# A chunked delta-rule scan: the end decay on the new values (ScalarE) in place of the keys (GpSimd)

## Chip, cores and metric

The kernel runs on one core of a Trainium2 chip. The metric is the device time of one execution in microseconds (us), the median of several. Engines are named PE (TensorE, matrix products), DVE (VectorE), ACT (ScalarE), POOL (GpSimd) and SP (SyncE, which issues most transfers).

## The reference

One layer of a hybrid backbone over 2048 latent tokens with a prefix of 256 context tokens: a mixer of two head groups (a chunked gating MLP and a bidirectional gated delta rule), and then a mixture of 16 experts. The part that matters here is the scan of the delta rule. Per direction, head (4 of 128) and chunk it carries a 128x128 state:

```python
g_last = gcum[..., -1]
k_g = kc * jnp.exp(g_last[..., None] - gcum)[..., None]

def step(state, xs):
    q_i, k_i, u_i, w_i, a_i, gl_i = xs
    v_new = u_i - w_i @ state
    o_i = q_i @ state + a_i @ v_new
    state = state * jnp.exp(gl_i)[..., None, None] + jnp.swapaxes(k_i, -1, -2) @ v_new
    return state, o_i
```

`k_g` is the key of a token times the decay from that token to the end of its chunk, a factor per token and head. In the product of keys and new values the token is the index that is summed over, so the factor may stand on either of the two.

## The kernel before

The kernel has four stages, written one after the other: the input projection with its convolution; the gating MLP, together with the preparation and the triangular solves of the delta rule; the scan, together with the output projection and the router; and the experts. The diff touches the scan alone (`scan`, L979 to L1038).

The scan works on chunks of 128 tokens, 18 of them (2 of context, 16 latent), in both directions at once: step s takes one chunk for the forward and one for the backward direction, so there are 18 steps and 36 scans. `scan` is a generator that yields between its products; `drive` (L866) takes one piece from each direction in turn, and, as a third generator, one from `finish` (L791 to L864), which assembles the inverse matrices for the next step out of what the solve has left (its products are L827, L835, L846, L848, L853 and L860; between them ACT and DVE evict, in L830, L839, L849, L854 and L863, and POOL multiplies by a mask in L822). From step 10 on each step also feeds `out_norm`, `out_proj` and `out_route` (L1040 to L1156) with two finished chunks.

For one chunk and one direction `scan` does this. Four tiles `kv` are loaded through SP (L986): keys `kr`, values `vr`, and transposed keys `kT` and queries `qT`; there are 12 buffers of the kind, and a buffer goes back when its last reader is done. POOL multiplies `kr` by EGK, the decay to the end of the chunk, one column per head (L988, 128x512, in place). PE multiplies `kT` with the state (L993), DVE subtracts (L995, one instruction per head), PE multiplies with the inverse UF (L1000), and DVE scales the result to the new values `vn` (L1006, or L1004 in the first step; one instruction for all heads). PE forms the state product of `kr` and `vn` (L1010, one matmul per head, two instructions to a matmul), and DVE adds it to the decayed state (L1016, or L1013 in the first step). For latent chunks PE then forms the queries' product with the old state (L1025) and the local one (L1029, which reads `vn` too), ACT copies (L1031) and DVE adds (L1033). The PSUM tiles `ks` of all these products share three buffers; `vn` has two.

The engines each work in the order of a list. A planner fixes it before the run: it takes the instructions in the order of the program, with a reckoning of the time that each takes, and places one of them on its engine when its inputs and a buffer are reckoned to be there. So PE's pieces of both directions, of `finish` and of the output projection are interleaved by the planner and not by the text of the program.

Beside the scan, in the same stretch of time: the last of the triangular solves (`solve`, L750 to L777) runs on DVE, 30 rounds of a product into `tmp` (L765) and a sum into `U` (L767) for each direction, all operands in SBUF; `load_wo` (L963) prepares the output weights, with two products per piece on POOL (L973 and L975) and a copy on ACT between them (L974); and the last chunks of the gating MLP (L660 to L713) use ACT, among others for a scaling by a column, four heads of 128x128 (L689). `rpow` (L164) is a small power on POOL.

## Time and profile before

| | us |
|---|---|
| median of 3 runs | 2490.56 |
| lowest, highest | 2490.39, 2495.03 |
| the profiled execution | 2486.87 |
| its span in the trace | 2485.1 |
| PE busy in the span | 2359.3 (95%) |
| DVE busy | 1577.9 (63%) |
| ACT busy | 1119.7 (45%) |
| POOL busy | 492.7 (20%) |

The times in the trace count from the start of the span. The scan's first products run at 758 us, its last at 1220 us. A row of the timeline gives the start, the length, the engine, the line and the operation, the tiles written and read, and how many instructions were merged into the row; in brackets stands the time that the engine was idle before it and what ended that. A busy share over the whole span is a mean over stages with different limits; a table by windows of the span shows each stage by itself. Such a row gives the window, its length, the busy time of PE, of PE's weight loads, of DVE, ACT and POOL (with the number of instructions), the clock that TensorE was granted as a share of 2.4 GHz, the mean busy share of the 16 DMA engines, and GB/s.

### The profile page before, as it was taken

What the parts mean: (1) busy time and instruction counts of PE and PEld (TensorE: products, weight loads), DVE (VectorE), ACT (ScalarE), POOL (GpSimd) and SP (SyncE); (2) the same over time, 40 slices, a digit from 0 to 9 for tenths busy, and PEclk for the clock granted to TensorE, in tenths of its full rate; (3) what the DMA queues carried; (4) which work ended last, traced back from release to release, by engine and by line L of the source; (5) the groups of instructions that cost most, each with busy time, mean ns of one, the idle gap of its engine ahead of it and who ended that gap; (6) DMA issues with size and microseconds to landing.
All of it is one profiled execution on the core that took longest, in us unless ns stands there. A gap on an engine that the chain in (4) does not pass through costs nothing.

```text
span 2485.1 us, 43121 instructions
## 1 busy us (share of the span) xinstructions
PE 2359.3 (95%) x16841; PEld 2156.1 (87%) x16841; DVE 1577.9 (63%) x3339; ACT 1119.7 (45%) x2008; POOL 492.7 (20%) x447
## 2 busy tenths in 40 slices
PE   7999999999988899999949999999999999999998
PEld 5999999887777888888838899999999999998888
DVE  7788755368779556576774556555565565556675
ACT  5554545567633343333332444444444444444553
POOL 1222212111102543232250101101111010011211
PEclk9999999999988999999978999999999999999999
DMA  9756735499856997555563667666676666668894
GB/s 288 229 191 220 239 123 171 144 290 299 260 120 195 264 270 231 189 188 174 174 189 111 204 187 224 195 206 205 204 221 195 212 213 197 208 208 262 311 304 161
DMA packets 487994, 526.59 MB, mean 212 GB/s; under 512 B 103887, under 2 KB 409880, under 8 KB 485742
## 3 DMA queue, kind: packets, MB, share of 16 engines
q1 hardware_dynamic: 470238, 463.27, 59.2%
q0 software_dynamic: 17120, 59.77, 8.3%
q8 instruction: 133, 2.18, 0.4%
q10 hardware_dynamic: 432, 0.79, 0.1%
q14 instruction: 71, 0.58, 0.1%
HBM read 400.45 MB, written 123.31 MB: 211 GB/s over the span
## 4 chain that ended last, share of the span: by engine, by line
PE 48%; DMA 9%; DVE 3%; issue 2%; ACT 2%; POOL 1%; SPq 0%; POOLq 0%; DVEq 0%; ACTq 0%
PE gu L196 7%; PE gu L195 7%; PE gu L194 7%; PE dn L194 4%; PE dn L195 4%; PE dn L196 4%; DMA xg<-f_rows,idx 4%; PE mx L194 2%; PE mx L196 2%; PE mx L195 2%; ACT wh L183 1%; PE xt L1381 1%; DVE wl L184 1%; DMA raw<-in_w_gate_dram 1%; DMA raw<-in_w_down_dram 1%
## 5 line engine op out<-in xcount | busy, mean ns | idle before, releaser
L184 DVE TENSOR_TENSOR wl<-raw,wh 128x2048 fp32r<-128x2048 f32 (+1 forms) x218 | 459.6, 2118 | 292.7 <-ACT wh L183 292.4
L194 PE MATMUL gu<-xS,wh 128*128 128x256 f32 x2048 | 581.3, 285 | 5.1 <-ACT wh L183 3.3
L196 PE MATMUL gu<-xS,wl 128*128 128x256 f32 x2048 | 579.2, 285 | 5.8 <-DVE wl L184 5.8
L195 PE MATMUL gu<-xS,wh 128*128 128x256 f32 x2048 | 580.9, 284 | 0.0
L183 ACT ACTIVATE wh<-raw 128x2048 fp32r<-128x2048 f32 (+1 forms) x218 | 381.6, 1771 | 360.6 <-DMA raw<-in_w_gate_dram 144.3
L194 PEld LDWEIGHTS gu<-xS,wh 128*128 128x128 f32 x2048 | 394.5, 193 | 7.5 <-ACT wh L183 4.2
L196 PEld LDWEIGHTS gu<-xS,wl 128*128 128x128 f32 x2048 | 393.1, 193 | 7.5 <-DVE wl L184 6.5
L195 PEld LDWEIGHTS gu<-xS,wh 128*128 128x128 f32 x2048 | 394.8, 193 | 1.1
L194 PE MATMUL pj<-aS,wh 128*128 128x258 f32 x832 | 236.6, 287 | 3.8 <-DVE y L460 2.4
L195 PE MATMUL pj<-aS,wh 128*128 128x258 f32 x832 | 238.5, 287 | 0.6 <-DVE aS L358 0.5
L196 PE MATMUL pj<-aS,wl 128*128 128x258 f32 x832 | 237.1, 286 | 0.8 <-DVE wl L184 0.8
L194 PE MATMUL dn<-wh,hS 128*128 128x512 f32 (+1 forms) x520 | 202.7, 390 | 0.0
L195 PE MATMUL dn<-wl,hS 128*128 128x512 f32 (+1 forms) x520 | 201.1, 387 | 0.0
L196 PE MATMUL dn<-wh,hS 128*128 128x512 f32 (+1 forms) x520 | 200.3, 386 | 0.0
L1458 POOL DMA_INDIRECT h_rows<-ye,idx x26 | 62.9, 2418 | 659.3 <-DVE ye L1421 567.0
L194 PEld LDWEIGHTS pj<-aS,wh 128*128 128x128 f32 x832 | 156.5, 189 | 5.2 <-ACT wh L183 1.8
L195 PEld LDWEIGHTS pj<-aS,wh 128*128 128x128 f32 x832 | 157.7, 190 | 1.3 <-DVE aS L358 1.0
L196 PEld LDWEIGHTS pj<-aS,wl 128*128 128x128 f32 x832 | 156.9, 189 | 1.3 <-DVE wl L184 1.1
L194 PE MATMUL uv<-wh,ast 128*128 128x512 f32 x384 | 155.7, 405 | 0.0
L196 PE MATMUL uv<-wh,ast 128*128 128x512 f32 x384 | 152.5, 397 | 0.0
L195 PE MATMUL uv<-wl,ast 128*128 128x512 f32 x384 | 152.2, 396 | 0.0
L1404 ACT ACTIVATE hS<-sgl 128x256 fp32r<-128x256 f32 x128 | 53.0, 414 | 184.1 <-DVE sgl L1402 183.9
(480 smaller groups left out, 4519.6 us busy)
## 6 DMA issues: line engine op xcount, KB each, us to landing
raw<-in_w_gate_dram SPq DMA_DIRECT2D x64, 1024.0 KB
raw<-in_w_up_dram SPq DMA_DIRECT2D x64, 1024.0 KB
raw<-in_w_down_dram SPq DMA_DIRECT2D x64, 1024.0 KB
kv<-kv SPq DMA_DIRECT2D x140, 256.0 KB
raw<-in_w_mod_dram SPq DMA_DIRECT2D x18, 1024.0 KB
a_sp<-aS SPq DMA_DIRECT2D x32, 512.0 KB
ast<-a_sp POOLq DMA_DIRECT2D x16, 1024.0 KB, 8.0
raw<-in_w_in_dram SPq DMA_DIRECT2D x12, 1024.0 KB
```

Of the source, the lines that this page charges most:

```text
L183: nc.scalar.activation(wh[:, ks, s:s + 256], raw[:, ks], AF.Copy)
L184: (lo_eng or nc.vector).tensor_tensor(wl[:, ks, s:s + 256], raw[:, ks], wh[:, ks, s:s + 256].bitcast(F32), op=OP.subtract)
L194: pace(nc.tensor.matmul(ps, ah, bh, start=(k == 0), stop=False), after)
L195: nc.tensor.matmul(ps, ah, bl, start=False, stop=False)
L196: return nc.tensor.matmul(ps, al, bh, start=False, stop=(k == nk - 1))
L1381: nc.tensor.transpose(ps[:, k2, hf * P:(hf + 1) * P], xg[:, hf, k * P:(k + 1) * P], ident)
L1404: nc.scalar.activation(hS[0][:, ff, :], sg_, AF.Copy)
L1458: nc.gpsimd.indirect_dma_start(out=h_rows, out_offset=bass.IndirectOffsetOnAxis(ap=idx[:, hf:hf + 1], axis=0), in_=ye[:, hf, :], in_offset ...
```

## The change

The product of the keys with EGK on POOL (L988) is gone. After `vn` is computed, four ACT instructions, one per head, copy `vn` into a new tile `vk` (128x512, one buffer) and multiply by the head's column of EGK on the way. The state product reads the unscaled keys and `vk`. The local product for the output (L1029) reads `vn`, as before. Nothing else is different.

```diff
--- before.py
+++ after.py
@@ -985,7 +985,6 @@
                 kv[i] = wkv.tile([P, H, P], F32, name="kv", bufs=12)
                 nc.sync.dma_start(kv[i], kv_d[t][:, i].rearrange("p (h i) -> p h i", h=H))
             kr, vr, kT, qT = kv
-            nc.gpsimd.tensor_tensor(kr, kr, EGK[:, d, ci:ci + H][:, :, None].to_broadcast([P, H, P]), op=OP.mult)
             if not first:
                 yield
                 ks = ps_s.tile([P, H, P], F32, name="ks")
@@ -1004,10 +1003,13 @@
                 nc.vector.scalar_tensor_tensor(vn, vps, -1.0, nb, op0=OP.mult, op1=OP.mult)
             else:
                 nc.vector.tensor_tensor(vn, vps, nb, op=OP.mult)
+            vk = wks.tile([P, H, P], F32, name="vk", bufs=1)
+            for h in range(H):
+                nc.scalar.activation(vk[:, h, :], vn[:, h, :], AF.Copy, scale=EGK[:, d, ci + h:ci + h + 1])
             yield
             sp = ps_s.tile([P, H, P], F32, name="ks")
             for h in range(H):
-                nc.tensor.matmul(sp[:, h, :], kr[:, h, :], vn[:, h, :], start=True, stop=True)
+                nc.tensor.matmul(sp[:, h, :], kr[:, h, :], vk[:, h, :], start=True, stop=True)
             Sn = wks.tile([P, H, P], F32, name=f"S{d}", bufs=2)
             if first:
                 mark[0] = nc.vector.tensor_copy(Sn, sp)
```

## Rows read from the trace of the kernel before

**Rows 1.** Timeline, DVE, then PE, 749 to 772 us.

```profile
750.47 0.55 DVE L765 TENSOR_TENSOR tmp<-U 96x108 f32<-96x108 f32 x2
750.94 1.40 DVE L767 TENSOR_TENSOR U<-U,tmp 96x108 f32<-96x108 f32 x2
...
753.27 1.45 DVE L765 TENSOR_TENSOR tmp<-U 96x150 f32<-96x150 f32 x2
...
755.47 0.89 DVE L767 TENSOR_TENSOR U<-U,tmp 96x228 f32<-96x228 f32 x1
...
757.39 1.50 DVE L765 TENSOR_TENSOR tmp<-U 96x184 f32<-96x184 f32 x2
...
767.94 0.87 DVE L830 TENSOR_TENSOR raw<-kk,m 64x256 f32<-64x256 f32 x2
...
758.23 1.95 PE L1000 MATMUL ks<-kv,raw 128*128 128x128 f32 x16
768.86 1.91 PE L835 MATMUL kk<-raw 128*128 128x32 f32 x8 [8.67 <-DVE raw L830]
```

**Rows 2.** Table by windows: length, busy us per engine, clock, DMA share.

```profile
764.00:778.00 14.00, 8.57 (x44) 8.07 (x45) 13.20 (x36) 3.33 (x10) 3.88 (x4) 0.51 0.14 41
820.00:840.00 20.00, 17.85 (x165) 16.90 (x164) 9.84 (x33) 8.37 (x19) 12.78 (x8) 1.00 0.93 265
840.00:860.00 20.00, 18.04 (x123) 16.47 (x121) 7.48 (x24) 6.63 (x18) 10.49 (x7) 0.74 0.93 267
1000.00:1040.00 40.00, 40.00 (x254) 34.05 (x254) 26.65 (x66) 15.72 (x35) 10.32 (x10) 1.00 0.64 208
```

**Rows 3.** Line L988: ns min/median/max; its busy time in a window.

```profile
L988 POOL TENSOR_TENSOR kv<-kv,EGK x36: 1029/1040/1231, 750.7 to 1169.9; 128x512 f32<-128x512 f32 x36
...
750.50:758.50 8.00, 4.58 (x4) 1.00 1.05 342
```

**Rows 4.** Line L1006: ns min/median/max, first and last start.

```profile
L1006 DVE TENSOR_TENSOR vn<-ks,NBET x34: 675/690/692, 785.2 to 1200.2; 128x512 f32<-128x512 f32 x34
```

**Rows 5.** Timeline of ACT at 770 to 776 us.

```profile
772.24 1.28 ACT L689 ACTIVATE gl<-gl,rvb 128x128 f32<-128x128 f32 x4 [0.31 <-POOL rvb L164]
```

**Rows 6.** Timeline: new values vn and the state products that read them.

```profile
785.25 0.69 DVE L1006 TENSOR_TENSOR vn<-ks,NBET 128x512 f32<-128x512 f32 x1
786.28 1.14 PE L1010 MATMUL ks<-vn,kv 128*128 128x128 f32 x8
...
796.01 0.69 DVE L1006 TENSOR_TENSOR vn<-ks,NBET 128x512 f32<-128x512 f32 x1
797.05 1.14 PE L1010 MATMUL ks<-vn,kv 128*128 128x128 f32 x8
...
815.64 0.68 DVE L1006 TENSOR_TENSOR vn<-ks,NBET 128x512 f32<-128x512 f32 x1
816.48 1.13 PE L1010 MATMUL ks<-vn,kv 128*128 128x128 f32 x8 [1.56 <-DVE vn L1006]
...
831.29 2.05 PE L1010 MATMUL ks<-vn,kv 128*128 128x128 f32 x16
...
983.37 0.68 DVE L1006 TENSOR_TENSOR vn<-ks,NBET 128x512 f32<-128x512 f32 x1
989.24 1.06 PE L1010 MATMUL ks<-vn,kv 128*128 128x128 f32 x8
```

**Rows 7.** Timeline of PE: the first step's two state products.

```profile
773.93 3.62 PE L1010 MATMUL ks<-vn,kv 128*128 128x128 f32 x16
```

**Rows 8.** Waits of PE, 775 to 960 us: total us, times, longest us.

```profile
PE ks L1029 <- ACT ot L1031: 4.6, 4, 1.9
```

**Rows 9.** Timeline at 826 to 833 us, ACT and PE.

```profile
828.43 1.06 ACT L974 ACTIVATE wh<-ft 128x1024 fp32r<-128x1024 f32 x1 [4.49 <-POOL ft L973]
...
829.70 0.41 PE L846 MATMUL lv<-ident,raw 64*64 64x64 f32 x4 [2.15 <-ACT raw L839]
```

## Prediction

> **What bounds the kernel now.** I read the table by stages first, then what each engine waits for, then the timeline around the lines that the diff touches. The change lies in the scan alone, 36 scans (18 steps, two directions) between 750 and 1210 us; the other 2,000 us see none of it.
>
> The scan has three parts. From 750 to about 772 us it overlaps the last triangular solve. There VectorE works without a gap, and TensorE stands still: after the matmuls at 758.23 us the next, at 768.86, waited 8.67 us for VectorE's L830, which stands in VectorE's queue behind the solve's L765 and L767 [rows 1]. From there to about 960 us (steps 0 to 11, 24 scans) neither TensorE nor the transfers leave much room: in 820 to 840 us TensorE is busy 17.85 of 20 us and the DMA engines 0.93 of the time, while ScalarE has 8.37 of 20 us [rows 2]. From 960 us on the output projection fills in, and TensorE is busy 40.00 of 40 us [rows 2]: what comes late to one matmul there is covered by others. So what the change does is decided in the first two parts.
>
> **Part by part.** Removed: 36 products on GpSimd, 1.04 us each in the median, 37 us in all [rows 3]. No row of TensorE's waits names GpSimd; these products are work beside the path, and the 37 us are no gain in themselves. The point is what they take from others: four of them run between 750.5 and 758.5 us beside the solve [rows 3], and VectorE's rows under them are stretched. A pair of L765 takes 0.55 us just before the first, and the pair of L767 with the same shape takes 1.40 under it; the pairs at 753.27 and 757.39 take 1.45 and 1.50, and a single one at 755.47 takes 0.89 [rows 1]. Against about 0.6 for a pair and 0.4 for a single (estimates from the 0.55) that is 0.85 + 0.85 + 0.9 + 0.5 = 3.1 us. VectorE has no idle time between them and L830, and TensorE stands waiting for L830, so all of it is on the path: -3.1 us. Next late there is still L830, since 5.6 us of the wait are left.
>
> The Trainium skill, GPSIMD Engine Reference, section 1 (Specifications), says that GpSimd shares its SBUF interfaces with VectorE, and that the contention concerns VectorE instructions with two SBUF inputs or in a two-port mode. If each of the 36 products cost VectorE 0.85 us on the path, the change would give back 31 us; the trace bears the rule out for the solve, whose inputs both lie in SBUF, and not beyond it.
>
> What VectorE does in the scan itself reads one input from PSUM, and its rows don't stretch: L1006 takes 675 to 692 ns in all 34 executions, beside a GpSimd product or not [rows 4]. So the gain ends with the solve, and I take no more than the 3.1 us.
>
> Added: per scan four ScalarE copies with a scale from a column. The nearest row is the same form in the stage before: L689, 128x128 from SBUF to SBUF with a column as scale, four in 1.28 us [rows 5]. 36 x 1.28 = 46 us of ScalarE, 31 of them in the 24 early scans. ScalarE is less than half busy there, so this is no bound as such; it counts as latency and as a place in a queue.
>
> As latency: the state product L1010 waited for VectorE's vn (L1006 or L1004); now it waits for vn and then vk. Its matmuls start about 0.23 us apart (16 instructions, two to a matmul, in 2.05 us less the tail of the last [rows 6]). With 0.1 us for each of the two hand-overs (an estimate, from the 0.16 between vn's end at 816.32 and the product at 816.48 that waited for it [rows 6]) the matmul of the fourth head could start 1.48 us after vn's end; unchanged, it starts 0.7 us after the first. So a product that starts 0.8 us or more after the end of vn loses nothing, if ScalarE is free. In the late part the distance is long: vn ends at 984.05, the product starts at 989.24 [rows 6]. In the early part three scans are closer: 785.94 and 786.28, 796.70 and 797.05, and the pair at 816 us [rows 6]. They are short of 0.8 by 0.5, 0.4 and 0.6: +1.5 us. The first step's two products run at half clock, 16 instructions in 3.62 us [rows 7], 0.45 us per matmul, and heads of vk every 0.3 us keep up with that; for the copies of L689 ahead of them in ScalarE's queue I take +0.5, between 0 and 1.3 (one group).
>
> vk has one buffer, so the second direction's copies wait until the first direction's product has read it. Where the two products run back to back, as the 16 instructions at 831.29 us [rows 6], the second starts later by nothing (released head by head) or by some 0.75 us (released as a whole); three such steps lie in the early part: 0 to 2.25, I take the middle, +1.1.
>
> As a place in the queue: ScalarE works in order and carries evictions that TensorE waits for. The largest sum of such waits in the early part is 4.6 us in 4 waits, for L1031 [rows 8]. If each of the four came behind one whole group of vk, that is +5 us; if none does, 0. vk takes 1.28 us of ScalarE twice in a step of 15 us, 1/6 of the time, so I stay near the lower end: +1.0.
>
> Moved: on GpSimd's queue the product waited for a transfer of keys; L973, L975, L822 and the small powers (L164) behind it may start sooner. Since no matmul waited for them, that is nothing, or a few tenths by way of VectorE. The keys' slot goes back when the state product has read it, as before; where that product is late, the transfer that takes the slot starts later on SP's queue, with what stands behind it there, and with the DMA engines at 0.93 nothing hides it. That is why I count the latencies in full. The order of instructions comes from a planner that reckons with costs of its own; with other instructions it may put TensorE's pieces in another order, which no row prices. That goes into the range.
>
> The sum is -3.1 + 0.5 + 1.5 + 1.1 + 1.0 = +1.0 us. The profiled execution took 2486.87 us (2485.1 in the span, 1.8 around it), and the median of the runs shown is 3.7 above it. On the median: 2491.5 us, no change.
>
> **The rivals.** Slower: TensorE starves at the state product, in steps 3 to 6. There ScalarE also runs L974, which waits for GpSimd and a transfer of weights: at 828.43 ScalarE had stood 4.49 us for it, L839 behind it was late, and TensorE's L846 waited 2.15 us [rows 9]. A group of vk behind such an L974 holds up the recurrence itself. For this speaks that ScalarE has one queue in order; against it, that GpSimd without the products may finish L973 sooner. Price: one wait like those 2.15 us. It decides from the point where TensorE's clock falls for it: in 840 to 860 us the granted clock is 0.74 of full, half the stretch at 1.2 in place of 2.4 GHz, and TensorE starts 123 matmul instructions, against 165 in the 20 us before [rows 2]; 42/165 x 20 = 5.1 us lost. Together 1.0 + 2.15 + 5.1 = +8.3: about 2499 us.
>
> Faster: the wait for L830 falls from 8.67 to 5.6 us, and the half-clock time behind it goes too (0.51 granted in 764 to 778 us [rows 2]). Then the 16 instructions of the first products take 2.05 us, as at 831.29, in place of 3.62 [rows 6, 7], 1.6 us less. The other 28 of the 44 instructions in that stretch would save 0.1 us each at the same ratio, 2.7 us, of which I count half, since they also wait for other engines: 1.3. If the planner covers the added latency but for the three tight scans, the sum is -3.1 - 2.9 + 1.5 = -4.5, and with some tenths by way of VectorE about 2485 us. By the skill's rule on the shared interfaces, cited above, this is the side on which I would be wrong. Against it: 5.6 us is still a long stop.
>
> No effect: VectorE's stretch comes back from another GpSimd instruction that moves into the place (L822, which also runs beside the solve), and vk is hidden. That gives 2490.5 us, inside the forecast's band.
>
> **How the numbers follow.** Forecast and no-effect case together 0.50, the slower rival 0.28, the faster one 0.22. What a measurement of this kernel can tell from no change is about 0.2%, 5 us, so these are also the chances of same (2485.6 to 2495.5), slower and faster. From the bounds above the forecast's own range is 2488.5 to 2498 (latencies and queue at their lower ends: -3.1 + 1.5; at their upper: -3.1 + 1.3 + 1.5 + 2.25 + 5). The range that should hold 8 in 10 reaches to both rivals and a little beyond, for a planner's order that no row prices: 2482 to 2502.
>
> **What would show it.** Right: rows of L765 and L767 near 0.6 us per pair at 750 to 758 us, and L835 some 3 us earlier; four ScalarE copies in 1.28 us per scan; state products in the early steps up to 0.6 us later behind vn, none of them in the late ones; GpSimd busy 37 us less. Wrong on the slow side: a wait of TensorE's L1010 for ScalarE of over 2 us, or one more stretch at half clock before 960 us. Wrong on the fast side: full clock from 764 us on, or an early part that is shorter by more than the 3 us. The prediction falls too if the late part, where I count nothing, changes its length by more than 2 us.

## The result, and the profile after

| | before | after |
|---|---|---|
| median, us | 2490.47 | 2523.15 |
| lowest, highest (4 runs each) | 2484.31, 2495.03 | 2509.06, 2528.39 |
| ratio of the times (95% interval) | | 1.0126 (1.0101 to 1.0150) |
| the profiled execution, its span | 2486.87, 2485.1 | 2528.39, 2526.6 |
| PE, DVE, ACT, POOL busy in the span | 2359.3, 1577.9, 1119.7, 492.7 | 2383.2, 1574.0, 1164.0, 461.0 |

The change makes the kernel 33 us slower; the forecast was no change, and the range ended at 2502. Line numbers of after: L992 is the product with the state, L999 the one with the inverse, L1005 the new values, L1008 the copies into `vk`, L1012 the state product, L1018 the new state, L1027 the queries' product, L1031 the local one.

Where the time went can be read from the starts of the steps (the first product with the state in each step; the last column is a mark at the start of the experts' stage, ACT's copy into `V`, L1239, in after L1241), in us of the span:

| | step 1 | step 2 | step 6 | step 11 | steps 2 to 11 | experts |
|---|---|---|---|---|---|---|
| before | 779.5 | 789.7 | 862.6 | 943.8 | 154.1 | 1269.9 |
| after | 777.2 | 787.1 | 876.4 | 979.0 | 191.9 | 1302.2 |

After is 2.3 and 2.6 us ahead at the first two steps, falls 38 us back in the nine steps from 2 to 11, and keeps 32 of it. So the loss lies where the prediction looked for it, in the early steps, and it is not one event: steps 6 to 10 last 19 to 23 us each, against 15 to 18 before. The two profiled executions differ by 41.5 us (2526.6 and 2485.1). The other 9 lie in the experts' stage, 1224.4 and 1215.2 us long, which the change doesn't touch and which lasts 1211 to 1224 us in the kept traces of all kernels.

First the stretch ahead of the scan. Timeline of after, DVE and then PE (the rows that answer to [rows 1]):

```profile
749.01 0.55 DVE L765 TENSOR_TENSOR tmp<-U 96x108 f32<-96x108 f32 x2
749.48 0.55 DVE L767 TENSOR_TENSOR U<-U,tmp 96x108 f32<-96x108 f32 x2
...
753.73 0.65 DVE L765 TENSOR_TENSOR tmp<-U 96x184 f32<-96x184 f32 x2
...
763.43 0.86 DVE L830 TENSOR_TENSOR raw<-kk,m 64x256 f32<-64x256 f32 x2
...
764.35 1.92 PE L835 MATMUL kk<-raw 128*128 128x32 f32 x8 [6.38 <-DVE raw L830]
```

No pair of the solve takes 1.4 or 1.5 us any more. From the start of the pair L765 with 96x108 elements to the start of L830 it is 14.42 us (763.43 - 749.01); before it was 17.47 (767.94 - 750.47), so 3.05 us are gone, where 3.1 were forecast. L830 as such comes 4.5 us earlier, since this execution was 1.5 us ahead when the stretch began. PE waits 6.38 us for it in place of 8.67.

Most of that is lost again in after's first step. From the start of L830 to step 1 it is 11.6 us before (767.94 to 779.5), 11.8 in e1, which has no copies, and 13.8 after (763.43 to 777.2). There the second direction's copies wait until the first state product, at half clock there, has read the one buffer:

```profile
775.00 1.28 ACT L1008 ACTIVATE vk<-vn,EGK 128x128 f32<-128x128 f32 x4 [3.14 <-PE ks L1012]
```

Then one step of the early part. Timeline of after, DVE, ACT and PE from 880 to 893 us:

```profile
880.38 1.42 DVE L1005 TENSOR_TENSOR vn<-ks,NBET 128x512 f32<-128x512 f32 x2
885.22 1.12 DVE L1018 SCALAR_TENSOR_TENSOR S<-S,ETO,ks 128x128 f32<-128x128 f32 x4 [3.41 <-PE ks L1012]
891.53 1.12 DVE L1018 SCALAR_TENSOR_TENSOR S<-S,ETO,ks 128x128 f32<-128x128 f32 x4 [5.19 <-PE ks L1012]
...
881.49 0.56 ACT L839 ACTIVATE raw<-lv 32x128 f32<-32x128 f32 x2
882.06 0.94 ACT L819 ACTIVATE raw<-UD 32x128 f32<-32x128 f32 x3
883.03 1.28 ACT L1008 ACTIVATE vk<-vn,EGK 128x128 f32<-128x128 f32 x4
884.33 0.30 ACT L819 ACTIVATE raw<-UD 32x128 f32<-32x128 f32 x1
884.66 0.55 ACT L839 ACTIVATE raw<-lv 32x128 f32<-32x128 f32 x2
885.23 1.28 ACT L1008 ACTIVATE vk<-vn,EGK 128x128 f32<-128x128 f32 x4
...
881.81 0.41 PE L846 MATMUL lv<-ident,raw 64*64 64x64 f32 x4 [0.74 <-ACT raw L839]
883.48 1.70 PE L1012 MATMUL ks<-vk,kv 128*128 128x128 f32 x8 [1.26 <-ACT vk L1008]
885.26 1.11 PE L848 MATMUL lv<-ident,raw 64*64 64x64 f32 x8
886.30 0.79 PE L1012 MATMUL ks<-vk,kv 128*128 128x128 f32 x2
886.89 1.91 PE L1027 MATMUL ks<-S,kv 128*128 128x128 f32 x8
888.60 1.06 PE L1012 MATMUL ks<-vk,kv 128*128 128x128 f32 x4
889.45 1.82 PE L1027 MATMUL ks<-S,kv 128*128 128x128 f32 x8
891.11 0.39 PE L1012 MATMUL ks<-vk,kv 128*128 128x128 f32 x2
```

Read it from vn to the state. The new values of both directions are there at 881.80. The first copies start at 883.03, behind five instructions of `finish` (L839, L819) that stand ahead of them in ACT's list. The second start at 885.23, behind three more of these; the first state product has read the one buffer just before, at 885.18, and ACT has no idle time there, so this step doesn't tell which of the two holds them. And PE has the last two instructions of the second state product at 891.11, because all 16 instructions of the queries' products L1027 stand between its pieces. The new state is complete at 892.65, 12.3 us after the start of vn. In a step of before, from the timeline of its DVE, the same way takes 6.7 us:

```profile
881.09 0.69 DVE L1006 TENSOR_TENSOR vn<-ks,NBET 128x512 f32<-128x512 f32 x1
882.87 0.69 DVE L1006 TENSOR_TENSOR vn<-ks,NBET 128x512 f32<-128x512 f32 x1 [1.09 <-PE ks L1000]
883.77 1.12 DVE L1016 SCALAR_TENSOR_TENSOR S<-S,ETO,ks 128x128 f32<-128x128 f32 x4 [0.20 <-PE ks L1010]
...
886.64 1.12 DVE L1016 SCALAR_TENSOR_TENSOR S<-S,ETO,ks 128x128 f32<-128x128 f32 x4
```

Below I call this way, from the start of the first vn to the end of the last state row, "values to state", and give its mean over the steps between 800 and 960 us: 6.9 us before, 13.0 after. The chain from state to state runs through it. The steps of one column vary: kernels that take about the time of before have 152 to 170 us for steps 2 to 11 in the table below, so a difference under some 15 us there tells little by itself.

It also costs clock. Table by windows of after (length, busy time of PE, its loads, DVE, ACT, POOL, granted clock, DMA share, GB/s), the same step in pieces, then two longer stretches; the last row is of before:

```profile
880.00:884.00 4.00, 2.00 (x18) 1.65 (x16) 1.75 (x4) 3.65 (x13) 0.42 (x1) 1.00 0.76 228
884.00:888.00 4.00, 3.92 (x22) 3.50 (x22) 1.12 (x4) 2.81 (x10) 0.00 (x0) 0.53 0.55 135
888.00:892.00 4.00, 4.00 (x25) 4.00 (x24) 0.47 (x2) 0.00 (x0) 0.00 (x0) 0.62 0.19 66
...
780.00:960.00 180.00, 156.09 (x1207) 146.79 (x1206) 84.28 (x274) 88.45 (x249) 54.38 (x38) 0.86 0.78 225
860.00:990.00 130.00, 112.80 (x840) 105.34 (x839) 56.82 (x184) 63.42 (x184) 26.86 (x23) 0.84 0.72 216
...
780.00:960.00 180.00, 165.29 (x1471) 154.66 (x1471) 106.88 (x347) 78.78 (x213) 80.26 (x64) 0.97 0.91 261
```

PE stands for half of 880 to 884, in two stops of 0.74 and 1.26 us, and then works about 7 us at half the clock; that comes back in each of the next steps, at 863.7, 884.2, 904.7, 925.1 and 945.6 us, 6.8 us each. From 755 to 1100 us half the clock was granted for 34 us before and for 75 us after. That is 41 us more, worth 20 us of products (half of 41).

The waits in 780 to 1000 us (in total, times, the longest): DVE and PE of after, then DVE of before:

```profile
DVE S L1018 <- PE ks L1012: 75.7, 19, 7.9
...
PE ks L1012 <- ACT vk L1008: 12.8, 8, 4.0
...
DVE S L1016 <- PE ks L1010: 7.3, 9, 1.7
```

DVE waits for the state product for 75.7 us, and for 7.3 before; PE itself shows only 12.8 us of waiting for `vk`. The rest of the lateness has no row of its own on PE: it is other work placed ahead.

### The profile page after: what moved, and what is told of

Read it like the earlier page. It is cut to its first block, busy times and chain, and to the rows that moved or that the text cites. A ratio compares the mean times of both kernels' runs of the same rounds, so it can differ in the third digit from the quotient of the medians.

```text
span 2526.6 us, 43229 instructions
## 1 busy us (share of the span) xinstructions
PE 2383.2 (94%) x16841; PEld 2179.9 (86%) x16841; DVE 1574.0 (62%) x3339; ACT 1164.0 (46%) x2152; POOL 461.0 (18%) x411
## 4 chain that ended last, share of the span: by engine, by line
PE 66%; DMA 14%; DVE 9%; issue 4%; ACT 4%; POOL 2%; SPq 1%; DVEq 0%; POOLq 0%; ACTq 0%
PE gu L196 6%; PE gu L195 6%; PE gu L194 6%; DMA xg<-f_rows,idx 4%; PE dn L194 4%; PE dn L195 4%; PE dn L196 4%; PE pj L195 4%; PE pj L194 4%; PE pj L196 4%; ACT wh L183 2%; PE mx L194 2%; PE mx L196 2%; PE mx L195 2%; PE ks L1027 1%
```

## The experiments

All ratios are against the kernel before, run on the same chip beside each. "Values to state" and "steps 2 to 11" are of the profiled execution. Differences between two kernels are told in medians; by the ratios they come out up to 4 us larger or smaller.

| kernel | median us | ratio (95%) | values to state | steps 2 to 11 |
|---|---|---|---|---|
| after | 2523.2 | 1.0126 (1.0101, 1.0150) | 13.0 | 191.9 |
| e1 no scaling at all | 2486.8 | 0.9983 (0.9966, 1.0000) | 7.0 | 154.9 |
| e2 keys scaled on ACT | 2490.9 | 0.9992 (0.9973, 1.0012) | 5.5 | 165.0 |
| e14 before + unread copies | 2490.1 | 0.9990 (0.9973, 1.0006) | 5.5 | 165.3 |
| e5 copy on DVE, beside vn | 2487.9 | 0.9984 (0.9964, 1.0004) | 6.9 | 158.8 |
| e6 copy on DVE, behind vn | 2505.9 | 1.0055 (1.0036, 1.0075) | 9.6 | 183.8 |
| e7 one short copy on ACT | 2514.9 | 1.0077 (1.0051, 1.0103) | 8.9 | 178.3 |
| e4 after + redundant products | 2512.5 | 1.0085 (1.0058, 1.0112) | 9.3 | 174.0 |
| e3 after, PE's order held | 2508.0 | 1.0069 (1.0044, 1.0094) | 8.8 | 179.4 |
| e9 after, ACT's order held | 2510.0 | 1.0077 (1.0056, 1.0097) | 8.0 | 176.9 |
| e13 after, no shared buffer | 2506.6 | 1.0053 (1.0036, 1.0069) | 9.1 | 174.6 |
| e8 both orders held | 2494.4 | 1.0014 (0.9997, 1.0031) | 6.2 | 170.3 |
| e15 both orders, one short copy | 2494.6 | 1.0005 (0.9987, 1.0023) | 7.1 | 162.2 |
| e16 both orders, no shared buffer | 2487.6 | 0.9978 (0.9957, 0.9998) | 6.1 | 166.5 |
| e10 before, part of after's order on PE | 2487.5 | 0.9975 (0.9954, 0.9996) | 6.7 | 158.6 |
| e12 before, state products first | 2490.4 | 0.9991 (0.9978, 1.0005) | 4.7 | 152.5 |
| e11 e5, state products first | 2496.0 | 1.0016 (1.0001, 1.0030) | 4.7 | 155.2 |
| e17 e5 with e10's order | 2489.4 | 0.9984 (0.9965, 1.0003) | 6.4 | 154.6 |

### Which part of the change costs: e1, e2, e14, e5

e1: the kernel before without the scaling.

```diff
-            nc.gpsimd.tensor_tensor(kr, kr, EGK[:, d, ci:ci + H]..., op=OP.mult)
```

> The kernel before without the product of the keys on GpSimd and with nothing in its place: the end decay is left out of the state, so the time is that of the work without it. It takes away the GpSimd work alone. Theory of the forecast: VectorE's solve is no longer held up beside it, the finishing product L835 comes 3 us earlier, and the time is 2487 us (about 3 below before). Rival, that GpSimd's product kept the planner's order in place and that taking it away is what costs: 2505 us or more. A scan step in the early part should last 15 to 17 us by the first and about 20 us by the second.

2486.8 us beside 2491.8 of before, 5 us less at the edge of what can be told. The stretch from L765 to L830 lasts 14.42 us, as in after; in e2, e5, e8 and e16, which have no product on GpSimd either, 14.35 to 14.43; in e10, e12 and e14, which have it, 17.20 to 17.22. So the removal is a small gain, and the solve has it: steps 2 to 11 take 154.9 us, as before.

e2: the keys scaled on ACT, four copies per scan, off the path.

```diff
-            nc.gpsimd.tensor_tensor(kr, kr, EGK[:, d, ci:ci + H]..., op=OP.mult)
+            for h in range(H):
+                nc.scalar.activation(kr[:, h, :], kr[:, h, :], AF.Copy, scale=EGK[:, d, ci + h:ci + h + 1])
```

> The kernel before with the keys scaled by four ScalarE copies in place of the product on GpSimd: the same ScalarE work as in the changed kernel (144 copies, 46 us), but on the keys, which are there long before, so that nothing stands between the new values and the state product. Theory, that the latency between vn and the state product is the cause: 2487 to 2493 us, as before or a little less, with steps of 15 to 17 us. Rival, that ScalarE's added load is the cause (its queue holds up the evictions that TensorE waits for): 2510 us or more, with steps near 20 us and falls of the clock as in the changed kernel.

The same amount of ScalarE work, 144 copies ahead of the path, costs nothing that can be told: 2490.9.

e14: before, plus the change's copies at their place, read by nobody.

```diff
                 nc.vector.tensor_tensor(vn, vps, nb, op=OP.mult)
+            vk = wks.tile([P, H, P], F32, name="vk", bufs=1)
+            for h in range(H):
+                nc.scalar.activation(vk[:, h, :], vn[:, h, :], AF.Copy, scale=EGK[:, d, ci + h:ci + h + 1])
```

> The kernel before, keys scaled on GpSimd and the state product from the new values, plus the 144 scaled copies on ScalarE at the place they have after the change, which nothing reads (they are extra work; the result is the reference's). Theory (the loss is the dependence: the state product behind the copies): the copies hang beside the path, time 2488 to 2498 us. Rival (the copies push ScalarE's evictions for the solve and the outputs back, and these hold the chain): 2505 us or more.

2490.1, no loss, though steps 2 to 11 are 11 us longer in this execution; the late part takes that up. Waits of DVE in e14, 780 to 1000 us:

```profile
DVE S L1019 <- PE ks L1013: 6.7, 9, 2.1
```

6.7 us for the state product, where after has 75.7. So the copies' load on ACT, and what they push back there, is not the cause of the 33 us; that the state product reads them is.

e5: the copy made on DVE from the product `vps`, ahead of vn, with one table for both factors (NEK is NBET times EGK; the lines that make it, and the form of the first step, are left out here).

```diff
+            vk = wks.tile([P, H, P], F32, name="vk", bufs=1)
+            nc.vector.tensor_tensor(vk, vps, NEK[:, d, ci:ci + H]..., op=OP.mult)
             nc.vector.tensor_tensor(vn, vps, nb, op=OP.mult)
-            for h in range(H):
-                nc.scalar.activation(vk[:, h, :], vn[:, h, :], AF.Copy, scale=EGK[:, d, ci + h:ci + h + 1])
```

> The kernel after, with the state product's scaled copy made on VectorE straight from the product vps (times one table that holds beta and decay together) and issued ahead of the new values, so that neither GpSimd nor ScalarE has a part in it and nothing stands between the new values and the state product; the copy keeps its one buffer. Same result as the reference's. VectorE gets 36 more instructions of about 0.7 us (25 us, on an engine busy 62% of the span). Theory (the loss is that a copy stands between the new values and the state product: 1.28 us for each direction, the queue of ScalarE in front of it, and the order in which the planner then lays TensorE's products): the state product can start as early as before the change, the early steps last 15 to 18 us as before the change, the stretch of steps 2 to 11 lasts 150 to 162 us, and the time is 2483 to 2496 us. Rival (the copy's one buffer, which the next direction's copy must wait for): the stretch stays over 170 us and the time over 2505 us.

2487.9, with one buffer still: the state product reads a copy here too, but a copy that doesn't come behind the new values, and the loss is gone.

### How long the copy takes: e6, e7

e6: one DVE instruction behind vn. e7: one ACT instruction behind vn, with one head's decay.

```diff
-            for h in range(H):
-                nc.scalar.activation(vk[:, h, :], vn[:, h, :], AF.Copy, scale=EGK[:, d, ci + h:ci + h + 1])
+            nc.vector.tensor_tensor(vk, vn, EGK[:, d, ci:ci + H]..., op=OP.mult)      (e6)
+            nc.scalar.activation(vk, vn, AF.Copy, scale=EGK[:, d, ci:ci + 1])          (e7)
```

> The kernel after, with the copy made by one VectorE instruction from the new values instead of four on ScalarE: it still stands between the new values and the state product and still has one buffer, but lasts about 0.7 us instead of 1.28 us and doesn't wait in ScalarE's queue. Same result as the reference's. Theory (time that the copy stands in the path, per direction, and the order that follows from it): half of the delay is left, so a part of the loss is: steps 2 to 11 last 158 to 178 us, one clock fall in some steps and none in others, time 2494 to 2512 us. Rival (only ScalarE's queue, with evictions ahead of the copy, is to blame): the time is that of before, 2485 to 2495 us. Second rival (any instruction between the new values and the state product costs the same, because the order alone decides): over 2515 us.

> The kernel after, with the four ScalarE copies of a direction as one instruction of 128x512 with one head's decay for all four heads (so the output isn't the reference's): the copy still stands in ScalarE's queue and in the path, but for less time (estimate 0.6 us instead of 1.28 us, from the 387 ns of one 128x128 copy, most of which is not its elements). Theory (time in the path): like the VectorE copy behind the new values, 2494 to 2512 us, steps 2 to 11 158 to 178 us. Rival (ScalarE's queue in front of the copy): little changes, 2512 us or more, since the copy still stands behind the same evictions.

The single ACT instruction takes 0.72 us (median of 36) and the one on DVE 0.68, for 1.28. That gives back 8 us on ACT (2514.9) and 17 us on DVE, where nothing of `finish` stands ahead of it (2505.9). For e7 the rival held: what stands ahead in ACT's list weighs more than the copy's own time. The planner changes the order in both, so neither isolates the duration: in the early steps of both the queries' products stand behind the state products, and there is a loss all the same. In e6 the second direction's copy starts within 0.1 us of the end of the first state product in every step from 815 to 960 us, so it is the buffer that holds it there. And four of e6's 36 copies, all in the early steps, take 1.63 to 2.84 us, 6.5 us more than four at the median. These run beside a product on POOL; DVE and POOL of e6, one of the four:

```profile
876.96 2.50 DVE L1007 TENSOR_TENSOR vk<-vn,EGK 128x512 f32<-128x512 f32 x1
...
876.57 2.34 POOL L973 TENSOR_TENSOR ft<-ft,xo 128x1024 f32<-128x1024 f32 x1
```

Each of the four ends 0.55 us behind the end of the product on POOL beside it (here 879.46 and 878.91): what the solve showed in before, with two inputs in SBUF, comes back on the path.

### The order: e3, e9, e8, e10

`pace` holds one instruction behind another in the list of its engine. e3: the queries' products behind the state products of both directions. e9: the copies of the next inverse (L819) behind the scaled copies last recorded, those of the step before. e8: both.

```diff
-                nc.tensor.matmul(sp[:, h, :], kr[:, h, :], vk[:, h, :], start=True, stop=True)          (e3, e8)
+                lsp[0] = nc.tensor.matmul(sp[:, h, :], kr[:, h, :], vk[:, h, :], start=True, stop=True)
...
-                    nc.tensor.matmul(qs[:, h, :], qT[:, h, :], S[d][:, h, :], start=True, stop=True)
+                    pace(nc.tensor.matmul(qs[:, h, :], qT[:, h, :], S[d][:, h, :], start=True, stop=True), lsp[0])
...
-                        nc.scalar.activation(UF[d][bs, :, bs], UD[bs, d], AF.Copy)                      (e9, e8)
+                        pace(nc.scalar.activation(UF[d][bs, :, bs], UD[bs, d], AF.Copy), lvk[0])
...
-                nc.scalar.activation(vk[:, h, :], vn[:, h, :], AF.Copy, scale=EGK[:, d, ci + h:ci + h + 1])      (e9, e8)
+                lvk[0] = nc.scalar.activation(vk[:, h, :], vn[:, h, :], AF.Copy, scale=EGK[:, d, ci + h:ci + h + 1])
```

> The changed kernel, with the queries' products with the old state placed behind the state products of both directions on TensorE (an order alone, no wait), as they stood before. In the changed kernel the planner put them between the heads of the second direction's state product, and VectorE's update of that state ended 5 us later for it. Theory, that this order is the main cost: at least two thirds of the 33 us come back, 2501 us or less, and the step falls from 20.3 to about 17 us. Rival, that the wait for vk and the falls of the clock behind it are the cost: the falls stay, one in each step, and the time is 2513 us or more.

> The kernel after with the order edge on ScalarE alone: the solve's copies of UF stand behind the scaled copies, and TensorE's order is left to the planner. Same result as the reference's. Without any edge: 2523 us; with TensorE's edge alone 2508.0; with both 2494.4. Theory (each engine's order takes a part of its own, about 15 us each): 2504 to 2513 us. Rival (TensorE's order matters only as long as the copies are late, so ScalarE's edge alone gives everything): 2492 to 2499 us. Second rival (ScalarE's edge gives nothing without TensorE's, since the second direction's state product stays behind the queries' products): 2516 to 2526 us.

> The kernel after with its order held on two engines and no work changed: on TensorE the queries' products stand behind the state products of both directions (as in the run with the order edge), and on ScalarE the copies of the next chunk's solve (out UF) stand behind the scaled copies. Same result as the reference's. With the first edge alone the time was 2508.0 us and steps 2 to 11 lasted 179.4 us. Theory (order and ScalarE's queue make up about half of the loss each, and the 1.28 us stays): the copies start 0 to 0.3 us after the new values instead of up to 2 us, steps 2 to 11 last 165 to 175 us, and the time is 2498 to 2506 us. Rival (ScalarE's queue costs nothing, what is left is the 1.28 us and the clock): as with the first edge alone, 2505 to 2513 us. Second rival (the solve's copies are now late themselves, and the next step waits for its triangular factor): over 2515 us.

15 us come back by PE's order, between theory and rival of e3; 13 by ACT's, as its theory had it; 29 by both, more than the theory of e8. Nothing was removed in e8: the same copies, the same dependence, and 1.0014 (0.9997 to 1.0031) of before. Timeline of e8, DVE and then ACT, one step:

```profile
879.11 1.29 DVE L1007 TENSOR_TENSOR vn<-ks,NBET 128x512 f32<-128x512 f32 x2
881.76 1.12 DVE L1020 SCALAR_TENSOR_TENSOR S<-S,ETO,ks 128x128 f32<-128x128 f32 x4 [1.36 <-PE ks L1014]
884.90 1.12 DVE L1020 SCALAR_TENSOR_TENSOR S<-S,ETO,ks 128x128 f32<-128x128 f32 x4 [2.02 <-PE ks L1014]
...
879.89 1.28 ACT L1010 ACTIVATE vk<-vn,EGK 128x128 f32<-128x128 f32 x4 [2.45 <-DVE vn L1007]
...
882.33 1.28 ACT L1010 ACTIVATE vk<-vn,EGK 128x128 f32<-128x128 f32 x4
883.51 2.04 ACT L820 ACTIVATE raw<-UD 32x128 f32<-32x128 f32 x8
```

ACT now waits for vn and copies 0.1 us behind the end of the first one (879.79); the eight L820 come behind both copies. Both states are there at 886.02 us, 6.9 us after the first vn began.

e10: is PE's order bad in itself? The kernel before, its second direction's state product held behind the first direction's queries' product, that is, behind eight of the 16 instructions that stand ahead of its last piece in after.

```diff
+            if d and lat and not first:
+                yield
...
-                nc.tensor.matmul(sp[:, h, :], kr[:, h, :], vn[:, h, :], start=True, stop=True)
+                mm = nc.tensor.matmul(sp[:, h, :], kr[:, h, :], vn[:, h, :], start=True, stop=True)
+                if d and lat and not first:
+                    pace(mm, lqs[0])
...
-                    nc.tensor.matmul(qs[:, h, :], qT[:, h, :], S[d][:, h, :], start=True, stop=True)
+                    lqs[0] = nc.tensor.matmul(qs[:, h, :], qT[:, h, :], S[d][:, h, :], start=True, stop=True)
```

> The kernel before, keys scaled on GpSimd, no copy anywhere, with the second direction's state products held behind the first direction's products for the queries, as the planner lays them after the change. No work is changed; same result as the reference's. Theory (TensorE's order by itself lengthens the chain from state to state by the queries' products, four of 0.25 to 0.5 us, and by what stands with them: 1 to 1.5 us in each of 10 steps): steps 2 to 11 last 163 to 175 us instead of 154, time 2499 to 2511 us. Rival (the order is harmless, only its combination with late copies costs): 2487 to 2496 us.

My theory fell here: 2487.5 us, not slower and, if anything, 0.25% faster. PE in one step of e10, and then the waits of its DVE, 780 to 1000 us:

```profile
915.79 1.06 PE L1030 MATMUL ks<-S,kv 128*128 128x128 f32 x8
...
917.78 0.49 PE L1013 MATMUL ks<-vn,kv 128*128 128x128 f32 x2
...
920.64 1.11 PE L1030 MATMUL ks<-S,kv 128*128 128x128 f32 x8
...
DVE S L1021 <- PE ks L1013: 14.9, 15, 2.2
```

No wait for the state product over 2.2 us. So half of after's order costs nothing where no copy stands behind the new values; the whole of it, with both directions' queries' products ahead, was not tried there. Behind the copies it costs 15 us (after and e3) or 16 (e9 and e8). My reading, argued and not shown, is that the planner then finds the queries' products ready first and sets them ahead, and the late product comes later still.

### The copies' own time and their buffer: e15, e13, e16

e15 is e8 with the one short copy of e7. e13 is after with the copy written over the values that its direction has used up; e16 is e8 with the same edit.

```diff
-            vk = wks.tile([P, H, P], F32, name="vk", bufs=1)
+            vk = vr                                                   (e13, e16)
```

> The run with both order edges (2494.4 us), with the four copies of a direction as one instruction of 128x512 with one head's decay for all four heads (so the output isn't the reference's): the copy takes 0.6 to 0.7 us of the path instead of 1.28 us. Theory (once the order is held, what is left is the copies' own time, about 7 us between this order with copies and the run with the copy beside the path): 2488 to 2493 us. Rival (what is left has another cause): 2493 to 2498 us as with four copies.

> The kernel after, with the scaled copy written over the values that its direction has just used up (vr) instead of into one buffer that both directions share: the second direction's copy need not wait until the first direction's state product has read. Same result as the reference's. Theory (the second direction's state product is late because its copy waits for the buffer, and the queries' products of the first stand around it): 10 us or more come back, time 2500 to 2514 us. Rival (the buffer is a small part: the copies wait longer for ScalarE's other work than for the buffer): 2516 to 2526 us.

> The kernel after with both order edges and with the copy written over its direction's used-up values: no work changed, same result as the reference's. Edges alone 2494.4 us, buffer alone 2506.6 us. Theory (all three act on the same gap, the second direction's state product coming late, so they don't add up below the level of before): 2489 to 2495 us. Rival (the buffer's share adds to the edges'): 2478 to 2486 us.

With the order held, a copy of 0.72 in place of 1.28 us changes nothing that can be told (2494.6 and 2494.4, the rival of e15). But the way hardly changes by it, because the state product starts before the fourth of the short copies is done. ACT and PE, the first direction in one step of e8 and then of e15:

```profile
897.61 1.28 ACT L1010 ACTIVATE vk<-vn,EGK 128x128 f32<-128x128 f32 x4 [0.24 <-DVE vn L1007]
...
898.07 1.36 PE L1014 MATMUL ks<-vk,kv 128*128 128x128 f32 x8 [0.38 <-ACT vk L1010]
...
886.35 0.72 ACT L1009 ACTIVATE vk<-vn,EGK 128x512 f32<-128x512 f32 x1 [0.24 <-DVE vn L1007]
...
887.12 1.16 PE L1013 MATMUL ks<-vk,kv 128*128 128x128 f32 x8 [0.70 <-ACT vk L1009]
```

From the start of the copy to the end of the product it is 1.82 us with four copies and 1.93 with one: the product starts 0.46 us behind the first of four and 0.77 behind the one. So e15 shows that one short copy is no better than four, and not that the copies' time is free; with the order held and no shared buffer (e16) that time costs nothing that can be told. The shared buffer alone is worth 17 us, and 7 us on top of the orders: with both orders and no shared buffer the change gives 2487.6, 0.9978 (0.9957 to 0.9998) of before, a little under the theory of e16. The three single gains (15, 13 and 17) add up to 45 and together return 36: they shorten the same way, and overlap. In e13 over half of the gain lies in steps 3 and 4 (9.5 us), where the second copies start 0.0 and 0.3 us behind their new values, and 4.0 and 7.0 in after; from 880 us on they start 3.3 to 3.4 us behind them in both kernels, since the same instructions of `finish` stand ahead. Waits in e16, 780 to 1000 us, DVE and ACT:

```profile
DVE S L1020 <- PE ks L1014: 15.2, 12, 3.3
...
ACT kv L1010 <- DVE vn L1007: 20.6, 13, 3.4
```

ACT now waits for the new values, 20.6 us in all, where in after the copies stand behind other work of ACT.

### The clock: e4

After, with four redundant products of keys and new values in front of the state product (their result is overwritten).

```diff
             for h in range(H):
+                nc.tensor.matmul(sp[:, h, :], kr[:, h, :], vn[:, h, :], start=True, stop=True)
+            for h in range(H):
                 nc.tensor.matmul(sp[:, h, :], kr[:, h, :], vk[:, h, :], start=True, stop=True)
```

> The changed kernel with four more matmuls per scan, of the keys with vn, ahead of the state product into the same PSUM tile (overwritten by it). They need no vk, so TensorE has 0.9 us more work per scan where it waited for vk, 32 us in all. Theory, that the stops at vk bring the clock down in each step and that the half-clock stretch costs most of it: the falls between 860 and 990 us (6 of 6.8 us in the changed kernel) go away, and the time is 2505 us or less in spite of the added work. Rival, that the clock is a by-product and the length of the chain is what costs: the time stays at 2520 us or rises by up to 20 us, with or without falls.

More work, 11 us less time, between the theory and the rival. Table by windows of e4, two of the stretches shown for after, and then its DVE in one step:

```profile
780.00:960.00 180.00, 170.46 (x1481) 160.08 (x1479) 90.21 (x293) 96.54 (x274) 55.78 (x40) 0.96 0.86 246
860.00:990.00 130.00, 122.82 (x1056) 113.90 (x1057) 64.38 (x206) 66.36 (x187) 28.70 (x25) 1.00 0.77 230
...
894.27 1.42 DVE L1005 TENSOR_TENSOR vn<-ks,NBET 128x512 f32<-128x512 f32 x2
...
902.10 1.12 DVE L1020 SCALAR_TENSOR_TENSOR S<-S,ETO,ks 128x128 f32<-128x128 f32 x4 [1.56 <-PE ks L1014]
```

The five falls are gone: from 860 to 990 us the clock stays at 1.00, where after has 0.84. Four steps from 874 us on last 16.1, 16.8, 16.8 and 20.6 us, in place of 20.1, 20.3, 20.4 and 22.6 of after, with about 2 us more work in each (a row of eight such instructions in e4 takes 1.16 us). The way from values to state in the step shown is 8.95 us (894.27 to 903.22), and 12.3 to 12.6 in steps 6 to 9 of after; what is between them, about 3.5 us, is near half of the 6.8 us at half the clock. The copies come as late as in after (2.0 and 3.7 us behind their values, there 2.0 and 3.4), and the 16 instructions of the queries' products still stand ahead of the last piece, though eight of them now ahead of the first state product. So in the steady steps the fall of the clock, and not the waiting alone, makes up a large part of the loss: some 3.5 of the 5.5 us that the way is longer than before. In steps 2 to 5 the filler doesn't help: they take 87 us, as in after (89).

### Looking for a better one: e12, e11, e17

e12: before with the solve's transposes (L846) and the queries' products behind both state products; e11: e5 with that order; e17: e5 with the order of e10.

```diff
+                        pace(nc.tensor.transpose(p3[a_, h, :], UF[d][a_, h, a_], ident[a_, a_]), lsp[0])   (e11, e12, beside e3's edge)
```

> The kernel before with the same order on TensorE, and nothing else: the solve's transposes and the queries' products behind the state products of both directions; keys scaled on GpSimd. Same result as the reference's. Theory (the order is worth something by itself, and GpSimd's products another 3 to 5 us at the start of the scan): 2480 to 2491 us, 2 to 6 us above the run with VectorE's copy and this order. Rival (the order of before is as good, since its waits in the early steps are few): 2489 to 2495 us, as before.

> The run with VectorE's copy beside the new values (2487.9 us, beside 2493.1 of before) with an order on TensorE: the solve's transposes and the queries' products stand behind the state products of both directions. Same result as the reference's. Theory (whatever stands between the new values and the next state costs step for step in the early steps): no product of the solve that waits for ScalarE stands in the chain any more, steps 2 to 11 last 145 to 155 us, time 2476 to 2488 us, 4 to 14 us under before. Rival (the solve is then late and the next step waits for its factor, or the clock falls in the gaps that the moved products leave): 2488 to 2500 us.

> VectorE's copy beside the path (2487.9 us) with the order on TensorE in which the second direction's state products stand behind the first direction's queries' products, and not the other way round (before with that order: 2487.5 us). Same result as the reference's. Theory (two gains of 3 to 5 us in different places, the solve ahead of the scan and the early steps, add up): 2481 to 2486 us. Rival (the gains are within what runs of one program differ by, and don't add): 2486 to 2493 us.

Both e11 and e12 have the shortest way from values to state, 4.7 us, the early part is hardly shorter for it (155.2 and 152.5), and the median of e11 is even 0.16% over before. The rival held in e11; e12 lies in both of its ranges. Why a shorter way gains nothing there is not shown; PE is busy for 160 (e11) and 168 us (e12) of 780 to 960, and for 165 in before. Nothing here is faster than before by more than 0.25%; e10 and e16 are the best, 0.25 and 0.22%, with intervals that just exclude no change. Of seventeen comparisons about one comes out so by chance, and e17, which joins e5's copy with e10's order, is no faster (0.9984, 0.9965 to 1.0003): there the rival held as well.

## Why the prediction was wrong

- **The gain at the solve: right.** -3.1 us forecast, 3.05 measured, and the same 2.8 to 3.1 between all kernels with the product and all without it. In after 2.2 us of it are lost again in the first step, where +0.5 was forecast: the second copies wait 3.14 us for the one buffer. The Trainium skill (GPSIMD Engine Reference, section 1, Specifications) has the contention for instructions with two SBUF inputs; e1 agrees, in so far as taking away all 36 products gives 5 us and not 31.
- **Added latency: the step that failed.** I took the order of PE's and ACT's lists as given and shifted single matmuls in it: a product that starts 0.8 us behind vn loses nothing, the tight ones lose 0.4 to 0.6. That asked for `vk` to start 0.1 us after vn. In after's step the first copy starts 1.9 us after its values (1.42 for two instructions, so the first half is there at about 881.1) and the second 3.4. "Values to state" grew by some 6 us a step, and not by 0.4 to 0.6 in three tight scans. Where the order is held the size was about right: in the step of e8 above the first state product ends 1.9 us behind its vn, and 1.3 in before where it waited for vn [rows 6], 0.6 us more.
- **The planner's order: named and not priced.** The prediction said that the order may change, that no row prices it, and gave it a few us at the ends of the range. It is the largest term: the two orders are worth 29 us (e8). Its size was not out of reach of the rows: ten early steps carry the recurrence, so a displacement of even 2 us in each is 20 us. The bound had to be taken per step, times the number of steps.
- **`vk`'s one buffer: right mechanism, mis-sized.** +1.1 us, 0 to 2.25; measured 7 us with the order held (2494.4 to 2487.6, with intervals that touch) and 17 us without. I counted it for three back-to-back steps, but it lies in the first step too, and with ACT's order held (e9) in each: from 850 to 960 us the second copies start there within 0.1 us of the end of the first state product. In after ACT's list mostly fills that time with other work; ACT stands idle for the buffer for only 3.4 us of 755 to 960 (`ACT vk L1008 <- PE ks L1012: 3.4, 2, 3.1`).
- **ACT's queue: counted in the wrong direction.** +1.0 us was for evictions behind `vk`; by e14 those cost nothing in the time of the whole. What cost was `vk` behind pieces of `finish`: taking L819 from in front of it gives back 13 us (e9).
- **The slower rival: right sign, one event instead of one per step.** It had PE starving at the state product and the clock falling for it, once, 2.15 + 5.1 us, behind L974 [rows 9]. Instead the copies stand behind L819 and L839, and half the clock is granted for 6.8 us in each of five steps running. The two rows that priced it don't belong together: behind the wait of 2.15 us, which ends at 829.70, the clock stays at 1.00 to 840 us [rows 2], and the fall in 840 to 860 us begins at 842.9, behind another stop, of 1.85 us, for L1031. The rival had 0.28, and the measured time lies 24 us above its price too.
- **The late part: nearly nothing, as forecast.** After is 35 us late at step 11 and 32 at the experts, so it changes by 3 us, where 2 was the bound beyond which I said the prediction falls. It can absorb more: e14 is 9 us late at step 11 (953.1) and 2 at the experts (1271.7), e16 9 and 1.
- **The faster rival: its condition didn't come.** PE's stop for L830 was shorter, 6.38 us, but the clock fell all the same: 0.61 is granted in 764 to 778 us of after.
- **GpSimd.** 37 us of products gone, POOL 32 us less busy (492.7 to 461.0), with no gain beyond the solve. PE's one wait for GpSimd in the trace of before is 0.2 us, for L406, outside the scan.

What stays open: the step from 2 to 3 lasts 23 to 26 us in after, e3, e4, e7, e8, e9, e13 and e16, and 17 in before and e1. e2 has 24 as well, without anything behind vn; in e16 PE waits 3.5 us there for an eviction (L850), in after 2.0 for DVE. I found no one cause. Nor is it shown how much of the 33 us is clock: half the clock for 41 us more makes 20 us at most, and e4's gain of 11 us is less the filler's own work. The time at half the clock alone doesn't order the kernels: e8 and e9 both have 51 us of it between 755 and 1100 us, and lie 16 us apart.

## What to carry to other kernels

An instruction put into a recurrence can cost far more than its own time where a planner or an in-order list decides what goes first: price its delay per step, times the steps, with the queue in front of it, the buffer behind it and the work that is ready earlier and will be set ahead. If the factor can be applied beside the path (e5, e2), or the order around it be held by hand (e8, e16), the same work costs nothing that these runs can tell (e8's interval ends at 1.0031). And short stops that recur in each step, here 2.0 us together, can go with a fall of the clock in each step: look at the granted clock in pieces of one step. They need not: before has stops of 1.56, 2.15 and 1.92 us at 815, 828 and 890 us and no fall behind them.

## What was new on the hardware

- The granted clock fell in step with the loop: in after half of it was granted for 6.8 us at 863.7, 884.2, 904.7, 925.1 and 945.6 us, once in each step of about 20.4 us, each time behind two stops of PE of 0.74 and 1.26 us. Redundant products in that place kept it at 1.00 and made the kernel 11 us faster.
- A ScalarE copy of 128x128 with a column as scale takes 0.387 us (median of 144), four in 1.28, and one of 128x512 with one column for all four 0.72. For the state product the single one was no gain (e15: 1.93 us from its start to the end of the product, 1.82 with four).
- A VectorE product with two inputs in SBUF, 128x512, takes 0.68 us, and 1.63 to 2.84 beside a GpSimd product of 128x1024; in all four cases of e6 it ended 0.55 us behind that one, which kept its 2.35 us. VectorE's L1006, with one input from PSUM, took 679 to 692 ns in the 13 cases that ran beside such products, and 675 to 692 in the other 21.
- Runs of one and the same kernel spread more than the first ones shown: before had 2482 to 2506 us in some 120 executions, so that a quarter of a per cent is at the limit of what these comparisons tell.
